# A two-layer recurrent decoder on one core: the second layer's recurrence in a new order of visits, its block transfers cut to the diagonal, and the weight loads on another queue

## The chip, the cores and the metric

The kernel runs on one core of a Trainium2 chip. The metric is the device time of one execution in microseconds: 2776.45 us as the median of three runs (2772.79, 2776.45 and 2785.57). One more execution was profiled; it took 2771.17 us, and its instructions span 2769.4 us.

## The reference, cut to what matters

Layer 0 (an RG-LRU and an HGRN2 group side by side) is left as it is. The change touches layer 1, RWKV-7 time mixing over 1024 positions, 2048 channels in 32 heads of 64, and the last projection with the final norm:

```
def rwkv7_scan(r, decay, k, v, kk, a):
    def step(state, inp):
        r_t, w_t, k_t, v_t, kk_t, a_t = inp
        s_kk = jnp.einsum("bhvk,bhk->bhv", state, kk_t)
        state = (state * w_t[:, :, None, :]
                 - s_kk[..., None] * (kk_t * a_t)[:, :, None, :]
                 + v_t[..., None] * k_t[:, :, None, :])
        y_t = jnp.einsum("bhvk,bhk->bhv", state, r_t)
        return state, y_t
...
    r = x_r @ w_r
    k_raw = x_k @ w_k
    v = x_v @ w_v
...
    y = rwkv7_scan(r, decay, k, v, kk, a)
    mean = jnp.mean(y, axis=-1, keepdims=True)
    var = jnp.mean(jnp.square(y - mean), axis=-1, keepdims=True)
    y = ((y - mean) * lax.rsqrt(var + GN_EPS)).reshape(bsz, s, RW_WIDTH) * lnx_g + lnx_b
    bonus = (jnp.sum(r * k * r_k, axis=-1, keepdims=True) * v).reshape(bsz, s, RW_WIDTH)
    out = ((y + bonus) * gate) @ w_o
```

## The kernel before, in words

The program runs layer 0, then the gates and low-rank parts of layer 1, and from about 1170 us of the profile on the part that the change touches. There the 1024 positions are cut into four quarters of 256 and the 32 heads into eight groups of four, which makes 32 **units**. In a unit the 256 positions of four heads are worked on as chunks of 64 positions, sixteen squares of 64 by 64 in all, so that the recurrence becomes small matrix products.

The work of one unit is written as generators, and each `yield` in them ends one *visit*:

- `stage_g` makes the unit's kr, r and v with 144 matmuls on 256 columns (names `g`). Every matrix value is a sum of two parts, so each product takes three matmuls. One piece of a weight matrix (512 KB, tile `wt`, names `w_kr`, `w_r`, `w_v`, later `w_o`) serves twelve matmuls; `piece` loads it ahead into one of five buffers.
- `stage_a` prepares decays and keys, forms the 128 by 128 products `pa`, masks them into `am`, stores the part that has to be inverted to DRAM (`nd`), and transposes (`pat`, `pbt`).
- `stage_i` reads these blocks back as `nb` (128 partitions of 32 by 32 values) and inverts the 32 blocks by 31 steps on VectorE (`itmp`, `xi`), about sixty short instructions a unit. The result goes to DRAM (`xd`) and comes back as `x32`, in the trace `x<-xd`.
- `stage_l` turns `x32` round on VectorE and joins the blocks to the inverse of a 64 by 64 square with two groups of 32 by 32 matmuls (`pl`, `pl2`).
- `stage_v` makes the centred v (`pvt`) and a first product with it (`pr0`).
- `stage_s` does the recurrence: `p1` in two halves, whose result is copied to `t1` and cast into `uv`; `p2` for even and odd chunks, added into `gm` and `rp` on VectorE; `ph` and `py`; and then four steps of the state, each with eight small matmuls into `ph` and eight into `py` and one VectorE instruction for the state (`sts`, at the last step `sper`).
- `stage_n` norms the result (sum `pvr`), multiplies by the gate and stores it (`y1d`).

The string `program` says in which order one turn of the loop makes these visits: a letter is a stage, the number behind it the distance of its unit from the current one, and a bare number so many sixths of `g` work (six matmuls each). TensorE's instructions are pinned to the order in which they are written. For the other engines a scheduler with its own timing sets the order, and each engine works through its own list in order. At the ends of the quarters `stage_x` makes the next quarter's inputs (names `xm`, `u`) beside the units.

PSUM has eight banks here: two for `g`, two for `pn`, `pb`, `pa`, `pat`, `pbt` (tag `m`), one for `pvt`, `pr0`, `pl`, `pl2` (tag `b`), one for `pvr`, `p1`, `p2` (tag `s`), and one each for `ph` and `py`.

A transfer is issued by the engine named before `.dma_start`, in that engine's order: SyncE (SP) issues the weights and all transfers of `nd`, `nb`, `xd`, `x32` and `y1d`; ScalarE (ACT) issues the reads of decays, a's and gates. `outs` is the last projection: it runs in two halves after the last `g`, with weights `w_o`.

Lines to follow: `pmap` 860, `pin` 873, `load_parts` 918, `piece` 924, `stage_a` 968, its stores of `nd` 1039, `stage_i` 1065 with its reads at 1070 and 1093, `stage_l` 1115, `stage_s` 1157 with the casts at 1169 and 1170, `stage_n` 1227, `outs` 1268, `program` 1351. Matmuls all carry the helper's line 882 (885 for transposes).

Of the kernel before, what the change touches and what calls it, by code (L numbers as in the profile page):

```python
# [19 lines left out]
P = 128  # L20
# [11 lines left out]
def trunk_kernel(ctx: ExitStack, tc: tile.TileContext, I, out, dbg=None):  # L32
# [822 lines left out]
    def eo(t):  # L855
# [6 lines left out]
        m="pn pb pa pat pbt",  # L862
        b="pvt pr0 pl pl2",
        s="pvr p1 p2",
# [8 lines left out]
    pinned = [None]  # L873

    def pin(i):
        if pinned[0] is not None:
            after(i, pinned[0])
        pinned[0] = i
        return i

    def mm(*args, **kw):
        return pin(PE.matmul(*args, **kw))  # L882

    def tr(*args):
        return pin(PE.transpose(*args))
# [30 lines left out]
    order_w = [(j, p_, q) for _ in range(4) for p_ in range(8) for j in range(3) for q in range(4)]  # L916
    loaded = []

    def load_parts(src, name):
        t = wp[0].tile([P, 2, 2, TQ], F32R, tag="wt", bufs=5, name=f"w_{name}")  # L920
        nc.sync.dma_start(t.bitcast(F32), src)
        return t

    def piece(i):

        while len(loaded) < min(i + 4, len(order_w)):
            j, p_, q = order_w[len(loaded)]
            loaded.append(load_parts(wd[p_][j][q], ("kr", "r", "v")[j]))
        return loaded[i][:, 0], loaded[i][:, 1]

    def weights1(dq, kp):
        ts = [load_parts(wod[dq][kp * 2 + q], "o") for q in range(2)]
        return [[t[:, w, k] for t in ts for k in range(2)] for w in range(2)]
# [34 lines left out]
    def stage_a(u):  # L968

        qt, pp_ = u["qt"], u["pp"]  # L970
        kr, rt = u["kr"], u["r"]
# [8 lines left out]
        yield  # L980
        k = spare(1, "k")
        for h_, c1 in two(pp_):
            S.activation(k[:, h_], a[:, h_], AF.Identity, scale=prm["c_k_a"][:, c1], bias=kam1[:, c1])
# [3 lines left out]
        after(S.activation(lamt[:, :, 1:65], ch(cum), AF.Exp, scale=-KAPPA), tabs)  # L987
# [3 lines left out]
        S.activation(li, cum, AF.Exp, scale=KAPPA)  # L991
# [9 lines left out]
        bh, bl = W1("ysq", dtype=F32R, name="bh"), W1("hsl", dtype=F32R)  # L1001
# [23 lines left out]
        nd = dp.tile([NCH * 2 * 4160], F32, tag="nd", bufs=2, name="nd")  # L1025
        ndw = nd.rearrange("(g h e x) -> g h e x", h=2, e=2, x=4160)
        for q in range(2):
# [6 lines left out]
            for h in range(2):  # L1034
# [3 lines left out]
                for e in range(2):  # L1038
                    nc.sync.dma_start(
                        ndw[q * 2:q * 2 + 2, h, 1 - e, 0:4096].rearrange("g (m t) -> m g t", t=64),  # L1040
                        am[q][ur[e], h, e::2, 0:64])
# [22 lines left out]

    def stage_i(u):
# [11 lines left out]
        for m in range(31):  # L1077
# [40 lines left out]
    def stage_l(u):  # L1118
# [36 lines left out]
    def stage_s(u):  # L1155
# [266 lines left out]
```

## Time and profile before

| what | value |
|---|---|
| median of three runs | 2776.45 us |
| the profiled execution | 2771.17 us, span 2769.4 us |
| TensorE busy over the span | 92% |
| VectorE, ScalarE, GpSimd busy | 62%, 44%, 24% |
| granted TensorE clock, mean | 0.972 |
| DMA | 566.50 MB in 531232 packets, 237745 of them under 512 B |

Busy shares are averages over stages with different limits. Matmuls overlap, so a busy TensorE is not one at its peak; what an edit is worth is read from the waits and the starts of single groups in the stage concerned. The share of the chain that ended last is 42% TensorE, 17% DMA and 15% VectorE.

### The profile page before, as it was taken

The numbers are of one execution on the slowest core, as the hardware profiler recorded it, in microseconds if no ns is written. First come the engines' busy times: TensorE is split into PE (matmuls) and PEld (weight loads), VectorE is DVE, ScalarE is ACT, GpSimd is POOL, SyncE is SP. The second block draws the span as 40 slices with busy tenths as digits, with TensorE's granted clock in tenths as the row PEclk, the third lists the DMA queues.
The fourth block names the chain that finished last, engine by engine and source line by source line (L and its number), as shares of the span: only waits on it lengthen the run. The fifth ranks groups of instructions, "written<-read, shape, count | busy, mean of one in ns | idle before, by whom it ended". The sixth has DMA issues, their size and how long they took to land.

```text
span 2769.4 us, 56914 instructions
## 1 busy us (share of the span) xinstructions
PE 2549.4 (92%) x22203; PEld 2214.3 (80%) x22203; DVE 1728.9 (62%) x4058; ACT 1226.1 (44%) x2439; POOL 654.7 (24%) x648
## 2 busy tenths in 40 slices
PE   7999999999999989997988999889998899998988
PEld 6777878788998766586887888778887788887988
DVE  5466566557657586245787676777767777677221
ACT  5466555555444455433345343453434434443221
POOL 2355444451116450111112011121111211110001
PEclk9999999999999999898999999999999999999999
DMA  6576666674564567685667576666765667666574
GB/s 202 170 254 223 217 212 224 222 255 141 190 192 137 178 198 223 207 293 177 191 210 225 183 221 191 201 203 210 227 198 189 208 204 221 202 211 186 170 266 151
DMA packets 531232, 566.50 MB, mean 205 GB/s; under 512 B 237745, under 2 KB 420242, under 8 KB 530962
## 3 DMA queue, kind: packets, MB, share of 16 engines
q1 hardware_dynamic: 473906, 481.50, 55.4%
q10 hardware_dynamic: 56192, 79.19, 8.7%
q8 instruction: 174, 2.85, 0.4%
q0 software_dynamic: 864, 2.18, 0.2%
q14 instruction: 96, 0.79, 0.1%
HBM read 428.52 MB, written 134.22 MB: 203 GB/s over the span
## 4 chain that ended last, share of the span: by engine, by line
PE 42%; DMA 17%; DVE 15%; issue 8%; ACT 6%; POOL 5%; SPq 4%; ACTq 0%; DVEq 0%; POOLq 0%
PE g L882 12%; PE pa L882 3%; DMA wd<-ht 3%; PE acc L882 3%; PE ph L882 3%; PE p L882 3%; POOL ht L382 2%; SPq L1093 2%; DVE xi L1086 2%; DVE itmp L1084 2%; PE py L882 2%; DMA y1d<-gt 2%; DMA x<-xd 2%; DMA nb<-nd 2%; SPq L1070 2%
## 5 line engine op out<-in xcount | busy, mean ns | idle before, releaser
L882 PE MATMUL g<-x,w_kr 128*128 128x256 f32 x1536 | 243.1, 301 | 8.2 <-DMA w_kr<-wd 8.2
L882 PE MATMUL g<-x,w_r 128*128 128x256 f32 x1536 | 247.1, 298 | 2.3 <-DMA w_r<-wd 2.3
L882 PE MATMUL g<-x,w_v 128*128 128x256 f32 x1536 | 232.7, 301 | 12.4 <-DMA w_v<-wd 12.3
L1086 DVE TENSOR_TENSOR xi<-xi,itmp 128x60 f32<-128x60 f32 (+21 forms) x864 | 222.5, 258 | 24.0
L382 POOL TENSOR_TENSOR ht<-ht 128x512 fp32r<-128x512 f32 x128 | 191.7, 1508 | 183.3 <-ACT ht L381 136.4
L1084 DVE TENSOR_TENSOR itmp<-xi,nb 128x60 f32<-128x60 f32 (+21 forms) x864 | 220.5, 255 | 22.5
L882 PEld LDWEIGHTS g<-x,w_kr 128*128 128x128 f32 x1536 | 206.6, 197 | 27.6 <-issue 19.5
L882 PEld LDWEIGHTS g<-x,w_v 128*128 128x128 f32 x1536 | 198.6, 194 | 32.7 <-DMA w_v<-wd 16.0
L882 PEld LDWEIGHTS g<-x,w_r 128*128 128x128 f32 x1536 | 199.6, 191 | 17.5 <-DMA w_r<-wd 2.5
L249 PE MATMUL acc<-wL_o,y 128*128 128x256 f32 x512 | 144.5, 286 | 7.1 <-DVE wL_o L183 7.1
L247 PE MATMUL acc<-wH_o,y 128*128 128x256 f32 x512 | 139.1, 285 | 4.2 <-ACT wH_o L182 2.0
L250 PE MATMUL acc<-wH_o,y 128*128 128x256 f32 x512 | 142.6, 283 | 0.0
L1074 POOL TENSOR_SCALAR xi<-eye 128x256 f32<-128x256 f32 x32 | 27.5, 861 | 469.0 <-DMA xd<-xi 388.6
L381 ACT CAST ht<-ht 128x512 fp32r<-128x512 f32 x128 | 78.2, 617 | 120.1 <-DMA wd<-ht 55.8
L882 PE MATMUL acc<-w_o,y 128*128 128x256 f32 x960 | 119.8, 288 | 7.3 <-DVE y L1263 4.2
L882 PEld LDWEIGHTS acc<-w_o,y 128*128 128x128 f32 x960 | 118.4, 196 | 8.6 <-DVE y L1263 4.9
L882 PE MATMUL p<-am,t 64*64 64x128 f32 x1024 | 73.6, 285 | 52.1 <-ACT uv L1170 52.1
L997 DVE TENSOR_TENSOR P<-r,lam 128x512 f32<-128x512 f32 x32 | 49.7, 1552 | 113.6 <-ACT r L953 113.6
L1036 DVE TENSOR_TENSOR am<-pa,rwm 128x512 f32<-128x512 f32 x128 | 85.4, 687 | 56.3 <-PE pa L882 56.1
L1217 ACT COPY ysb<-py 128x512 f32<-128x512 f32 x32 | 18.8, 587 | 229.2 <-PE py L882 229.2
L833 POOL TENSOR_TENSOR x<-xm,x 128x512 fp32r<-128x512 f32 x48 | 65.6, 1371 | 210.2 <-ACT x L832 210.2
L199 PE MATMUL gr<-g,wL_g 128*128 128x512 f32 x256 | 105.5, 412 | 9.4 <-DVE wL_g L183 9.3
(391 smaller groups left out, 6614.9 us busy)
## 6 DMA issues: line engine op xcount, KB each, us to landing
w_kr<-wd SPq DMA_DIRECT2D x128, 512.0 KB, 6.7
w_r<-wd SPq DMA_DIRECT2D x128, 512.0 KB, 4.1
w_v<-wd SPq DMA_DIRECT2D x128, 512.0 KB, 3.9
wd<-ht SPq DMA_DIRECT2D x96, 512.0 KB, 3.6
w_o<-wod SPq DMA_DIRECT2D x64, 512.0 KB, 3.4
wod<-ht SPq DMA_DIRECT2D x32, 512.0 KB, 3.6
wst_o<-in_ab_w_out_dram SPq DMA_DIRECT2D x64, 256.0 KB, 3.2
wst_g<-in_c_w_g_dram SPq DMA_DIRECT2D x64, 256.0 KB, 3.0
```

The lines of the kernel that those rows point to most:

```text
L199: PE.matmul(ps, l[k], xh[k], start=False, stop=(k == NK - 1))
L247: PE.matmul(o, yH[kt][:, ts_], wh[j], start=(first and tb % 2 == 0), stop=False, skip_group_check=True)
L249: PE.matmul(o, yH[kt][:, ts_], wl[j], start=False, stop=False, skip_group_check=True)
L250: PE.matmul(o, yL[kt][:, ts_], wh[j], start=False, stop=last, skip_group_check=True)
L381: i = S.copy(hl[:, 0].bitcast(F32R), st)
L382: G.tensor_tensor(hl[:, 1].bitcast(F32R), st, hl[:, 0], op=sub)
L833: G.tensor_tensor(xl, x, xh.bitcast(F32), op=sub)
L882: return pin(PE.matmul(*args, **kw))
L1036: V.tensor_tensor(am[q][:, h, :, 0:P], pa.rearrange("p (c t) -> p c t", t=P), rwm.unsqueeze(1).broadcast_to([P, 4, P]), op=mult)
L1070: nc.sync.dma_start(nb[32 * g:32 * g + 32], u["nd"].rearrange("(p x) -> p x", x=2080)[:, 0:2048].rearrange("p (m s) -> p m s", s=64)[:, :, ...
L1084: V.tensor_tensor(t3, xi[:, 0:n, m:m + 1].broadcast_to([P, n, w]), nb[:, m:m + 1, m + 1:32].broadcast_to([P, n, w]), op=mult)
L1086: V.tensor_tensor(xi[:, 0:n, m + 1:32], xi[:, 0:n, m + 1:32], t3, op=add)
```

## The change

- **Order of visits.** The string `program` is new. Small matmuls that stood alone between pieces of `g` work now stand in a row: both halves of `p2`, `ph`, `py` and the first state step; a state step with one half of `pa`, twice; the last state step with `pr0`. With the two groups of `stage_l` these are six places a unit in which matmuls use parts of the array; before there were twelve. In return `g` stands in longer pieces.
- **PSUM.** `p1` and `p2` get two names each, one on tag `s` and one on tag `b`; `pvt` moves to tag `m`.
- **Casts.** Both casts of `p1` into `uv` are done on ACT; before, one was on VectorE.
- **Blocks.** Only the 32 by 32 diagonal blocks are stored to `nd` (eight stores of 16 KB in place of eight of 32 KB), and `nb` is read in one transfer of 512 KB with rows of 4 KB in place of four transfers of 128 KB with rows of 128 B. The number of a square within `xb` and the squares' places in `am` follow.
- **Weight loads.** All of them, `w_o` too, go through `piece`, are issued by ACT in place of SP, and run five pieces ahead in place of four.
- **ACT's order.** Some ACT work of `stage_a` must stand behind the last copy of `pl` (`behind`).
- **Norm.** The store of `y1d` becomes a visit of its own, made one turn later.
- The last unit's `g` work is all done in its own turn.

```diff
@@ -859,9 +859,9 @@
-        m="pn pb pa pat pbt",
-        b="pvt pr0 pl pl2",
-        s="pvr p1 p2",
+        m="pn pvt pb pa pat pbt",
+        b="p1b p2b pr0 pl pl2",
+        s="p1a p2a pvr",
@@ -870,19 +870,25 @@
...
+    pinned = {}
+
+    def pin(f):
...
+    mm, tr = pin(PE.matmul), pin(PE.transpose)
+    last_copy = []
+
+    def behind(i):
+        for c in last_copy:
+            after(i, c)
@@ -913,24 +919,18 @@
-    order_w = [(j, p_, q) for _ in range(4) for p_ in range(8) for j in range(3) for q in range(4)]
+    order_w = [(wd[p_][j][q], ("kr", "r", "v")[j]) for _ in range(4) for p_ in range(8) for j in range(3) for q in range(4)]
+    order_w += [(wod[dq][q], "o") for _ in range(2) for dq in range(4) for q in range(8)]
...
-    def load_parts(src, name):
-        t = wp[0].tile([P, 2, 2, TQ], F32R, tag="wt", bufs=5, name=f"w_{name}")
-        nc.sync.dma_start(t.bitcast(F32), src)
-        return t
-
     def piece(i):
 
-        while len(loaded) < min(i + 4, len(order_w)):
-            j, p_, q = order_w[len(loaded)]
-            loaded.append(load_parts(wd[p_][j][q], ("kr", "r", "v")[j]))
+        while len(loaded) < min(i + 5, len(order_w)):
+            src, name = order_w[len(loaded)]
+            t = wp[0].tile([P, 2, 2, TQ], F32R, tag="wt", bufs=5, name=f"w_{name}")
+            nc.scalar.dma_start(t.bitcast(F32), src)
+            loaded.append(t)
         return loaded[i][:, 0], loaded[i][:, 1]
-
-    def weights1(dq, kp):
-        ts = [load_parts(wod[dq][kp * 2 + q], "o") for q in range(2)]
-        return [[t[:, w, k] for t in ts for k in range(2)] for w in range(2)]
 
     def stage_g(u):
@@ -978,17 +978,20 @@
...
-            S.activation(k[:, h_], a[:, h_], AF.Identity, scale=prm["c_k_a"][:, c1], bias=kam1[:, c1])
+            behind(S.activation(k[:, h_], a[:, h_], AF.Identity, scale=prm["c_k_a"][:, c1], bias=kam1[:, c1]))
...
-        after(S.activation(lamt[:, :, 1:65], ch(cum), AF.Exp, scale=-KAPPA), tabs)
+        i = S.activation(lamt[:, :, 1:65], ch(cum), AF.Exp, scale=-KAPPA)
+        after(i, tabs)
+        behind(i)
...
-        S.activation(li, cum, AF.Exp, scale=KAPPA)
+        behind(S.activation(li, cum, AF.Exp, scale=KAPPA))
@@ -1022,8 +1025,8 @@
 
-        nd = dp.tile([NCH * 2 * 4160], F32, tag="nd", bufs=2, name="nd")
-        ndw = nd.rearrange("(g h e x) -> g h e x", h=2, e=2, x=4160)
+        nd = dp.tile([32 * 1024], F32, tag="nd", bufs=2, name="nd")
+        ndw = nd.rearrange("(q c e u m t) -> q c e u m t", q=2, e=2, u=2, m=32, t=32)
         for q in range(2):
             yield
             pas = [pu("pa") for h in range(2)]
@@ -1035,10 +1038,11 @@
                 pa = pas[h]
                 V.tensor_tensor(am[q][:, h, :, 0:P], pa.rearrange("p (c t) -> p c t", t=P),
                                 rwm.unsqueeze(1).broadcast_to([P, 4, P]), op=mult)
-                for e in range(2):
-                    nc.sync.dma_start(
-                        ndw[q * 2:q * 2 + 2, h, 1 - e, 0:4096].rearrange("g (m t) -> m g t", t=64),
-                        am[q][ur[e], h, e::2, 0:64])
+            for e in range(2):
+                for b in range(2):
+                    r0 = ur[e].start + 32 * b
+                    nc.sync.dma_start(ndw[q, :, 1 - e, b].rearrange("c m t -> m c t"),
+                                      am[q].rearrange("p h (g e) t -> p (h g) e t", e=2)[r0:r0 + 32, :, e, 32 * b:32 * b + 32])
         u.update(pt=pt, am=am, bv=bv, nd=nd, lc=lc)
 
@@ -1062,13 +1066,13 @@
...
 
         nb = W1("nb", bufs=1, shape=(P, 32, 32))
-        for g in range(4):
-            nc.sync.dma_start(nb[32 * g:32 * g + 32], u["nd"].rearrange("(p x) -> p x", x=2080)[:, 0:2048].rearrange(
-                "p (m s) -> p m s", s=64)[:, :, 0:32])
+        nc.sync.dma_start(nb.rearrange("p m s -> p (m s)"),
+                          u["nd"].rearrange("(p x) -> p x", x=1024).unsqueeze(0).broadcast_to([4, 32, 1024]))
@@ -1088,6 +1092,7 @@
                 yield
         nc.sync.dma_start(xd.rearrange("g c x t -> g (c x t)").rearrange("g (b y) -> (g b) y", y=256),
                           xi.rearrange("p j t -> p (j t)"))
+        yield
...
@@ -1133,12 +1138,11 @@
...
-                ce = (c // 2) * 2 + h
-                mm(pl[rb, c * 32:c * 32 + 32], am[ce // 4][ra, c % 2, ce % 4, 32:64], x1[ra, c, :],
+                mm(pl[rb, c * 32:c * 32 + 32], am[c // 4][ra, c // 2 % 2, c % 2 * 2 + h, 32:64], x1[ra, c, :],
...
             rb = slice(ur[h].start + 32, ur[h].start + 64)
-            S.copy(x1[rb].rearrange("p c t -> p (c t)"), pl[rb, 0:256])
+            last_copy[:] = [S.copy(x1[rb].rearrange("p c t -> p (c t)"), pl[rb, 0:256])]
         yield
@@ -1161,19 +1165,19 @@
-            p1 = pu("p1")
+            p1 = pu(("p1a", "p1b")[q])
             for j in range(4):
-                mm(p1[:, j * P:(j + 1) * P], xb[:, q * 4 + j, :], ar[:, :, q * 4 + j, :], start=True, stop=True)
+                mm(p1[:, j * P:(j + 1) * P], xb[:, q * 4 + j % 2 * 2 + j // 2, :], ar[:, :, q * 4 + j, :], start=True, stop=True)
             p1 = p1.rearrange("p (j s c) -> p j s c", s=2, c=64)
             S.copy(t1[:, q * 4:q * 4 + 4], p1[:, :, 0])
-            V.tensor_copy(uv[q][ur[0], 0], p1[ur[0], :, 1])
-            S.copy(uv[q][ur[1], 1], p1[ur[1], :, 1])
+            for e in range(2):
+                S.copy(uv[q][ur[e], e], p1[ur[e], :, 1])
             yield
 
         gm = W1("gm", bufs=1, shape=(P, NCH, 64))
         rp = W1("rp", bufs=1, shape=(P, NCH, 64))
         for e in range(2):
-            p2 = pu("p2")
+            p2 = pu(("p2a", "p2b")[e])
             for g in range(4):
...
-            if e == 0:
-                ph = pu("ph")
...
-                py = pu("py")
...
-                yield
+
+        ph = pu("ph")
...
+        py = pu("py")
...
+        yield
@@ -1242,6 +1245,7 @@
...
+        yield
         nc.sync.dma_start(y1d[qt // 2][pp_ // 2][2 * (pp_ % 2):2 * (pp_ % 2) + 2, :,
                                                  (qt % 2) * TQ:(qt % 2 + 1) * TQ].rearrange("i p t -> p i t"),
...
@@ -1274,16 +1278,15 @@
...
             for kt in range(16):
-                if kt % 4 == 0:
-                    wh, wl = weights1(dq, kt // 4)
-                j = kt % 4
+                wh, wl = piece(12 * n + (hf * 4 + dq) * 8 + kt // 2)
...
                     o = acc[tb // 2][:, (tb % 2) * 256:(tb % 2) * 256 + 256]
-                    mm(o, yH[kt][:, ts_], wh[j], start=(kt == 0 and tb % 2 == 0), stop=False, skip_group_check=True)
-                    mm(o, yH[kt][:, ts_], wl[j], start=False, stop=False, skip_group_check=True)
-                    mm(o, yL[kt][:, ts_], wh[j], start=False, stop=(kt == 15), skip_group_check=True)
+                    mm(o, yH[kt][:, ts_], wh[:, j], start=(kt == 0 and tb % 2 == 0), stop=False, skip_group_check=True)
+                    mm(o, yH[kt][:, ts_], wl[:, j], start=False, stop=False, skip_group_check=True)
+                    mm(o, yL[kt][:, ts_], wh[:, j], start=False, stop=(kt == 15), skip_group_check=True)
...
@@ -1349,8 +1352,8 @@
     program = """
-        a2 s0 2 i1 v1 i1 s0 1 i1 a2 1 i1 s0 1 s0 1 i1 s0 1 v1 1 i1 s0 1 a2 1 i1 s0 1 i1 a2 1 i1 s0 1 i1 s0 n0 1
-        a2 1 i1 a2 1 a2 i2 1 n0 l1 1 i2 a3 l1 3 i2 l1 i2 1 i2 1 a3 i2 1""".split()
+        s0 s0 v1 i1 1 a2 i1 1 n-1 i1 s0 s0 s0 s0 i1 1 i1 1 i1 1 s0 a2 i1 1 i1 1 1 s0 a2 i2 i1 1 i2 1 i2 1 s0 v1
+        i2 a3 2 n0 a2 a2 i2 2 i2 a2 n0 l1 i2 1 i2 2 a3 i2 1 l1 i2 1 1 l1 1 a3 i2 2""".split()
...
-            if s + d == n - 1:
-                left = 21
...
                 fill(k)
-                if s + d == n and left < 97:
+                if s + d == n and left < 99:
...
-                go(t[0], s + int(t[1]))
+                go(t[0], s + int(t[1:]))
...
             prepare(4)
+    go("n", n - 1)
...
-    fill(96 - 80)
+    fill(96 - 83)
```

The next pieces show what stands in a row on an engine, before and after. They are of the twentieth unit.

First TensorE, from the product with the inverse on. `p` and `p1a`, `p1b` are the halves of `p1` where they read `ar` and `xb`; `p`, `p2a`, `p2b` with `am` and `t` are `p2`; "..." stands for matmuls of `g` and for the other half of `pb`. Before:

```order
L882 MATMUL p_22604<-ar,xb 128x128 x4
...
L882 MATMUL pvt<-cent,v 128x128 x4
L882 MATMUL p_22646<-ar,xb 128x128 x4
...
L882 MATMUL pb<-hsl,bdr 128x512
...
L882 MATMUL p_22686<-am,t_22603 64x128 x8
...
L882 MATMUL ph<-uv,am 64x64 x16
L882 MATMUL py<-am,uv 64x64 x16
...
L882 MATMUL p_22749<-am,t_22603 64x128 x8
```

and now:

```order
L878 MATMUL p1a<-ar,xb 128x128 x4
L878 MATMUL p1b<-ar,xb 128x128 x4
L878 MATMUL pvt<-cent,v 128x128 x4
...
L878 MATMUL pb<-bl,bdr 128x512
...
L878 MATMUL p2a<-am,t_22561 64x128 x8
L878 MATMUL p2b<-am,t_22561 64x128 x8
L878 MATMUL ph<-uv,am 64x64 x16
L878 MATMUL py<-am,uv 64x64 x16
L878 MATMUL ph<-sper,gm 64x64 x4
L878 MATMUL py<-rp,sper 64x64 x4
```

The halves of `p1` have become neighbours, on two banks, and `p2`, `ph`, `py` and the first state step are one run without `g` between them.

Next ACT at the same place. `t` and `uv` are the copies out of `p1`, `sqa` the norm of the keys, `w_kr` and `w_r` weight loads. Before:

```order
L1002 CAST bh<-r 128x512
L953 COPY v<-g 128x512
L1008 ACTIVATE sqa<-sqa 128x512
L1168 COPY t_22603<-p_22604 128x256
L1009 ACTIVATE sqa<-sqa 128x512
L1170 COPY uv<-p_22604 64x256
L1234 DMA gt<-gd 128x512
L1106 COPY uv<-pvt 64x256 x4
L1168 COPY t_22603<-p_22646 128x256
L987 ACTIVATE lam<-cum 128x8x64
L1170 COPY uv<-p_22646 64x256
```

and now:

```order
L931 DMA w_kr<-wd_210 128x1024
L1005 CAST bh<-r 128x512
L1011 ACTIVATE sqa<-sqa 128x512
L953 COPY v<-g 128x512
L931 DMA w_r<-wd_211 128x1024
L1012 ACTIVATE sqa<-sqa 128x512
L1172 COPY t_22561<-p1a 128x256
L1174 COPY uv<-p1a 64x256 x2
L1172 COPY t_22561<-p1b 128x256
L1174 COPY uv<-p1b 64x256 x2
L1237 DMA gt<-gd 128x512
L1111 COPY uv<-pvt 64x256 x4
```

Six copies out of `p1` stand together ahead of those out of `pvt`, and weight loads stand among ACT's own work.

Last VectorE, from the end of the inverse to the next one. `itmp` and `xi` are steps of the inverse, `x` is `x32`, `sts` and `sper` the state. Before:

```order
L1084 TENSOR_TENSOR itmp<-xi,nb 128x8
L1086 TENSOR_TENSOR xi<-xi,itmp 128x8
L1221 TENSOR_TENSOR sts<-ph,lc 128x128
L1036 TENSOR_TENSOR am<-pa,rwm 128x4x128 x2
L1221 TENSOR_TENSOR sts<-ph,lc 128x128
L1221 TENSOR_TENSOR sper<-ph,lc 128x128
L997 TENSOR_TENSOR P<-r,lam 128x512
L1124 STREAM_TRANSPOSE x_22454<-x_22399 32x256 x2
L1129 COPY xb<-x_22399 32x8x32 x2
```

and now:

```order
L1088 TENSOR_TENSOR itmp<-xi,nb 128x8
L1090 TENSOR_TENSOR xi<-xi,itmp 128x8
L1224 TENSOR_TENSOR sper<-ph,lc 128x128
L1129 STREAM_TRANSPOSE x_22398<-x_22204 32x256 x2
L1134 COPY xb<-x_22204 32x8x32 x2
L1000 TENSOR_TENSOR P<-r,lam 128x512
```

Behind the last step of the inverse (`xi` of 128x8) stood six instructions that need other engines and `P`; now the last state step alone stands there, and `P` stands behind the transposes.

## Rows read from the trace of the kernel before

**Rows 1.** The page: busy us, share of the span, instructions.
```profile
PE 2549.4 (92%) x22203; PEld 2214.3 (80%) x22203; DVE 1728.9 (62%) x4058; ACT 1226.1 (44%) x2439; POOL 654.7 (24%) x648
```

**Rows 2.** Busy time by stretch: PE, PEld, DVE, ACT, POOL, clock, DMA share, GB/s.
```profile
1428.30:1573.50 145.20, 120.65 (x1382) 108.25 (x1380) 103.66 (x304) 65.61 (x144) 30.91 (x30) 0.92 0.65 201
1573.50:1775.80 202.30, 190.56 (x2348) 169.68 (x2347) 147.39 (x459) 82.02 (x180) 25.02 (x30) 1.00 0.68 206
1775.80:1873.80 98.00, 83.54 (x949) 74.34 (x948) 74.63 (x210) 49.45 (x108) 26.04 (x24) 0.91 0.66 204
2121.00:2218.00 97.00, 83.23 (x957) 73.88 (x956) 73.65 (x204) 47.80 (x104) 25.82 (x24) 0.93 0.63 196
```

**Rows 3.** The key norm's first VectorE instruction, by line, 1310 to 2463 us.
```profile
L1007 DVE TENSOR_SCALAR sqa<-pn x28: 682/684/694, 1310.8 to 2462.4; 128x512 f32<-128x512 f32 x28
```

**Rows 4.** The same line, 1573.5 to 1775.8 us.
```profile
L1007 DVE TENSOR_SCALAR sqa<-pn x6: 683/684/694, 1573.5 to 1775.8; 128x512 f32<-128x512 f32 x6
```

**Rows 5.** TensorE's waits, 1170 to 2770 us: total us, times, longest.
```profile
PE p L882 <- ACT uv L1170: 63.3, 42, 5.4
PE pl L882 <- DVE x L1124: 44.0, 52, 11.6
```

**Rows 6.** TensorE's waits, 1573.5 to 1775.8 us.
```profile
PE p L882 <- ACT uv L1170: 6.5, 7, 1.1
PE pl L882 <- DVE x L1124: 2.6, 10, 0.4
PE g L882 <- DMA w_v<-wd: 2.6, 4, 1.4
```

**Rows 7.** TensorE's waits, 1428.3 to 1573.5 us.
```profile
PE p L882 <- ACT uv L1170: 12.3, 5, 5.4
PE pl L882 <- DVE x L1124: 8.1, 2, 8.0
PE g L882 <- DMA w_v<-wd: 2.0, 1, 2.0
```

**Rows 8.** TensorE's timeline: start us, us, instruction, count.
```profile
1576.94 0.96 PE L882 MATMUL g<-x,w_kr 128*128 128x256 f32 x6
1577.74 0.40 PE L882 MATMUL pb<-bh,bdr 128*128 128x512 f32 x1
...
1591.27 0.98 PE L882 MATMUL g<-x,w_r 128*128 128x256 f32 x6
1592.17 0.45 PE L882 MATMUL ph<-sts,gm 64*64 64x64 f32 x8
1592.46 0.40 PE L882 MATMUL py<-rp,sts 64*64 64x64 f32 x8
1592.79 0.98 PE L882 MATMUL g<-x,w_r 128*128 128x256 f32 x6
```

**Rows 9.** The chain that ended last, 1536 to 1552 us: start us, us.
```profile
1540.23 2.23 DMA xd<-xi
...
1542.51 0.59 SPq L1093
...
1545.10 4.25 DMA x<-xd
...
1549.48 0.44 DVE x L1124
```

**Rows 10.** The tile uv, 1573.5 to 1775.8 us: ns min, median, max.
```profile
L1169 DVE COPY uv<-p x10: 427/427/428, 1575.1 to 1741.8; 64x256 f32<-64x256 f32 x10
L1170 ACT COPY uv<-p x10: 366/366/367, 1575.6 to 1742.2; 64x256 f32<-64x256 f32 x10
```

**Rows 11.** A transfer that ACT issues, line 1234: ns of the issue.
```profile
L1234 ACTq DMA_DIRECT2D gt<-gd x32: 326/326/495, 1174.7 to 2584.4; - x32
```

**Rows 12.** The page's DMA issues: count, KB each, us to landing.
```profile
w_kr<-wd SPq DMA_DIRECT2D x128, 512.0 KB, 6.7
nb<-nd SPq DMA_DIRECT2D x128, 128.0 KB, 3.0
```

**Rows 13.** SP's own waits, 1170 to 2770 us.
```profile
SPq L921 <- PE g L882: 575.2, 219, 12.4
```

More of the change, by code (lines that the diff above doesn't have):

```diff
@@ L870, in pu, with g @@
         return pp[0].tile([P, 512], F32, tag=pmap[use], bufs=pcnt[pmap[use]], name=use)
[L873 to L885, printed above, removed]
+    pinned = {}
+    def pin(f):
+        def g(*args, **kw):
+            i = f(*args, **kw)
+            e = i.ins.engine
+            if e in pinned:
+                after(i, pinned[e])
+            pinned[e] = i
+            return i
+        return g
+    mm, tr = pin(PE.matmul), pin(PE.transpose)
[3 more added lines that the diff above has]
+            after(i, c)
     xb = W1("xb", shape=(P, 8, P))
@@ L970, in stage_a @@
         qt, pp_ = u["qt"], u["pp"]
-        kr, rt = u["kr"], u["r"]
+        kr = u["kr"]
         cum = W1("cum", bufs=2)
@@ L980, in stage_a @@
         yield
+        rt = u["r"]
         k = spare(1, "k")
         for h_, c1 in two(pp_):
-            S.activation(k[:, h_], a[:, h_], AF.Identity, scale=prm["c_k_a"][:, c1], bias=kam1[:, c1])
+            behind(S.activation(k[:, h_], a[:, h_], AF.Identity, scale=prm["c_k_a"][:, c1], bias=kam1[:, c1]))
         V.tensor_tensor(k, kr, k, op=mult)
@@ L1000, in stage_a @@
             V.scalar_tensor_tensor(rt[:, h_], rt[:, h_], prm["c_r_k"][:, c1], k[:, h_], op0=mult, op1=mult)
-        bh, bl = W1("ysq", dtype=F32R, name="bh"), W1("hsl", dtype=F32R)
+        bh, bl = W1("ysq", dtype=F32R, name="bh"), W1("hsl", dtype=F32R, name="bl")
         S.copy(bh, rt)
@@ L1185, in stage_s @@
             yield
-            if e == 0:
-                ph = pu("ph")
-                for c in range(NCH):
-                    for h in range(2):
-                        j = (c // 2) * 2 + h
-                        mm(ph[hr[h], cs(c)], am[c // 4][:, h, c % 4, P:192], uv[c // 4][:, c % 2, j % 4, :],
-                           start=(c == 0), stop=False, skip_group_check=True)
-                py = pu("py")
-                for c in range(NCH):
-                    for h in range(2):
-                        j = (c // 2) * 2 + h
-                        mm(py[hr[h], cs(c)], uv[c // 4][:, c % 2, j % 4, :], am[c // 4][:, h, c % 4, 64:128],
-                           start=(c == 0), stop=False, skip_group_check=True)
-                yield
+        ph = pu("ph")
+        for c in range(NCH):
+            for h in range(2):
+                j = (c // 2) * 2 + h
+                mm(ph[hr[h], cs(c)], am[c // 4][:, h, c % 4, P:192], uv[c // 4][:, c % 2, j % 4, :],
+                   start=(c == 0), stop=False, skip_group_check=True)
+        py = pu("py")
+        for c in range(NCH):
+            for h in range(2):
+                j = (c // 2) * 2 + h
+                mm(py[hr[h], cs(c)], uv[c // 4][:, c % 2, j % 4, :], am[c // 4][:, h, c % 4, 64:128],
+                   start=(c == 0), stop=False, skip_group_check=True)
+        yield
         sts = W1("sts", bufs=1, shape=(P, 4, 2, 64))
@@ L1276, in outs @@
             for kt in range(16):
-                if kt % 4 == 0:
-                    wh, wl = weights1(dq, kt // 4)
-                j = kt % 4
+                wh, wl = piece(12 * n + (hf * 4 + dq) * 8 + kt // 2)
+                j = kt % 2
                 for tb in range(4):
```

## The prediction

> **What bounds the kernel now.** I read the page first: TensorE is busy for 92% of the span, VectorE for 62%, ScalarE (ACT) for 44% [rows 1]. That makes TensorE the engine to watch, and the question is where it is not at its own pace. For that I took stretches [rows 2] and counted units in them with one instruction that stands once in each unit. It starts 28 times between 1310.8 and 2462.4 us, so 27 units take 1151.6 us, 42.65 us each [rows 3]. Where no inputs of a next quarter are made, five units take 202.3 us, 40.5 each, at a clock of 1.00 [rows 4]. In the three stretches beside the making of inputs the clock is 0.91 to 0.93, a mix of the two levels 1.2 and 2.4 GHz, and seven units take 145.2 + 98.0 + 97.0 = 340.2 us, 48.6 each [rows 2]. The other 20 units are then (1151.6 - 340.2) / 20 = 40.6.
>
> The waits come next. TensorE stands before `p1`, whose bank is held by the casts of `uv`, for 63.3 us in all, and before the products with the inverse (`pl`) for 44.0 us [rows 5]. In the five undisturbed units these two and a late weight make 6.5 + 2.6 + 2.6 = 11.7 us, 2.3 a unit [rows 6]; in the first stretch 12.3 + 8.1 + 2.0 = 22.4 us in three units, 7.5 each [rows 7]. VectorE is busy for 147.39 / 5 = 29.5 us of an undisturbed unit and ACT for 82.02 / 5 = 16.4 [rows 2], so no engine but TensorE is near its limit by work alone. VectorE is near it by a chain, below.
>
> **Visits.** A group of six `g` takes 0.80 us from its start to that of the following `pb` in full tiles, and 0.90 us to that of a `ph` in parts of the array; the way back, from `py` to `g`, is 0.33 us, where `ph` to `py` is 0.29 [rows 8]. One visit thus costs 0.10 going in and 0.04 coming out, and I take 0.15 in all. Twelve visits become six: 6 x 0.15 = 0.9 us a unit. But four changes of shape now stand inside a visit (`p2` to `ph`, `py` to a state step, a state step to `pa` twice), each between 0 and 0.10, so the term lies between 0.5 and 0.9. I take 0.7. A rule of the Trainium skill speaks against it (TensorEngine Tiling (Array Packing), Key Properties): changing the tiling mode, not only the tile, drains TensorE, so modes would be counted and not visits, 24 changes before and 16 now, and by half a visit's 0.15 for each change the term would be 8 x 0.075 = 0.6. The rows bear the drain out going in, by the 0.10; for a change inside a visit none of them has a price.
>
> **Banks and casts.** The halves of `p1` and of `p2` get two banks, so the second half need not wait for the copies of the first; the same waits cannot come back at `p1`, they can only move to the first user of either bank. The cast that leaves VectorE frees 2 x 0.427 = 0.86 us there a unit and costs ACT 2 x 0.366 = 0.73 [rows 10]. ACT has 24 us a unit free, which hides that as long as copies do not queue up; uncovered it is the 0.73.
>
> **Weight loads.** Twelve issues a unit go from SP to ACT. An issue takes ACT 0.326 us [rows 11], so 12 x 0.326 = 3.9 us a unit, hidden in the same free time: 16.4 + 0.7 + 3.9 = 21.0 of 40. Such a load lands 6.7 us after its issue [rows 12], and TensorE works through a piece, two groups of six, in 40.5 / 12 = 3.4 us on the mean and in 2 x 0.80 = 1.6 us where `g` stands unbroken [rows 8]. Four pieces in between are 13.5 us and 6.4 us, so there is ample time on the mean and none to spare in a dense row of `g`. SP now stands 575.2 us in 219 waits for `g` to free a buffer [rows 13], with the blocks' transfers queued behind. This standing moves to ACT, where copies, casts and exponentials are queued behind it. It does no harm where these need matmuls that come later in TensorE's order than the one waited for, which holds for copies out of `p1`, `pvt` and `ph`; it does harm to the decays' exponentials, whose users are VectorE and GpSimd. I price it at 0, with the upper end in the rival on ACT.
>
> **Blocks.** Eight stores of half the size, no price. Four reads of `nb` with 3.0 us to landing become one of 512 KB, for which the nearest rows are that 3.0 and the 6.7 of a weight piece of equal size [rows 12]. It lies between the reads of `x32`, ahead of it on SP, and the first step of the inverse; VectorE meanwhile has the transposes, `P` and the norm. I take 4.5 and cost 0; at 6.7, uncovered by 2 us, it would add 2 us to VectorE's loop. The Trainium skill has a rule against just this form (DMA: Bandwidth & Descriptors, Rules for kernel authors): an outermost broadcast of c copies keeps the whole transfer on at most c engines, here 4 of 16. With its 27 GiB/s an engine that is 128 KB in about 4.5 us of moving alone (estimate), and the read would land at some 6.5 us, near the upper end; no run here shows a read of that form.
>
> **What is late next.** The chain shows what VectorE's order now leaves bare. From the start of the inverse's way to DRAM to the first transpose of what came back it is 1549.48 - 1540.23 = 9.25 us: 2.23 for the store, issues of 0.59, 4.25 for the reads [rows 9]. Before, VectorE had two masks, three state steps and `P` to do in that time; now only `sper` stands there, and it waits for the transposes with all else behind them. So VectorE's loop is 29.5 - 0.86 + 9.25 = 37.9 us. TensorE's own is 40.5 - 2.3 - 0.7 = 37.5. The two meet, and neither is reached exactly, since each still waits for the other at the masks and the state steps. I add 0.9 to the longer (a choice, of the size of one wait in [rows 6]) and take 38.8 a unit, 1.7 less than 40.5. In the stretches VectorE's work is 103.66 / 3 = 34.6, 74.63 / 2 = 37.3 and 73.65 / 2 = 36.8 [rows 2]; with 9.25 - 0.86 added that is 43.0, 45.7 and 45.2, by units 44.4. I take 44.5, 4.1 less than 48.6. The norm's store a turn later, `behind` and the last projection's loads are hidden by TensorE's `g` and cost 0.
>
> **The sum.** 20 x 1.7 = 34 and 7 x 4.1 = 29. The remaining five units, at both ends, have 0.7 x 5 = 3.5 from visits, and their waits: by rows 6 and 7 the 27 units hold some 20 x 1.3 + 7 x 4.1 = 55 of the 63.3 and 20 x 0.5 + 7 x 2.7 = 29 of the 44.0, which leaves 23, and half of that, 12, goes. Together 78.5 us off the profiled execution's 2771.2: 2693 us. That execution lies 5.3 us under the median of the runs, 0.2%, which I don't add.
>
> **Rivals.**
> - VectorE takes the place entirely: its loop keeps the 9.25 us and waits for masks and state steps besides. Units go to 39.8 and stretches to 47.0: 20 x 0.7 + 7 x 1.6 + 12 = 37 us less, 2734 us. For it speaks that nothing fills the gap; against it that its work alone is far from 40.
> - The chain gets shorter, since no weight load stands between its transfers on SP. At the 3.0 of a small read in place of 4.25 and one issue of 0.59 it is 2.23 + 0.59 + 3.0 = 5.8 us. Then TensorE's 37.5 decides (20 x 3.0 = 60) and the stretches fall to 41.0 (7 x 7.6 = 53): with 15.5 at the ends 128 us less, 2643 us. Against it: the four reads still follow each other at 0.59.
> - Slower: ACT is held in its order. `bh` waits for VectorE's `r`, and a weight load and the copies out of `p1` stand behind it. In a dense row of `g` a load has no time to spare, so a hold of 4 us makes TensorE 4 us late. At once a unit that is 32 x 4 = 128 us against a gain of 78: 2821 us. It decides from 78 / 32 = 2.5 us a unit on. Against it: ACT is idle for half of a unit.
> - The change does not do what it says: waits only move from `uv` to the transposes, visits cost by changes of shape and not by their number, and units stay at 40.5: 2771 us.
>
> **How the numbers follow.** The forecast has 0.50, VectorE in its place 0.17, the shorter chain 0.15, ACT's hold 0.10, no change 0.08. What a measurement of this kernel can tell from no change is about 0.5%, 14 us. The first three are faster: 0.82; 0.08 within; 0.10 slower. The range leaves out ACT's hold, half of the no-change case and the far end of the shorter chain: 2630 to 2765. It holds the 2 us of a late `nb` (32 x 2 = 64 us, 2757).
>
> **What would show it.** Right: the rows `p` behind `uv` are gone or below 10 us; units of about 39 us where the clock is full and about 44.5 in the stretches; VectorE's longest wait is for the reads of `x32`, several us in each unit; six `g` to a group in parts still at 0.90. Wrong: TensorE's waits for `w_kr`, `w_r`, `w_v` of over 20 us (ACT held); waits of VectorE for `nb` of over 1 us a unit (the broadcast); TensorE waiting for `pl` as long as before, with units above 40 (no net gain); or units below 38 with VectorE hardly waiting (the shorter chain).

## The result: 7% slower, and VectorE stands for the blocks

The changed kernel takes 2973.74 us (median of four runs, 2962.09 to 2979.2), the one before 2776.81 (its profiled execution counted in). The ratio is 1.0699, 95% interval 1.0674 to 1.0725. The forecast was 2693 us. The profiled execution took 2962.09 us, 190.9 more than that of before.

First the page, the line of busy time, and of the chain that ended last the shares by engine and the first shares by line:

```profile
PE 2562.4 (87%) x22203; PEld 2255.3 (76%) x22203; DVE 1645.2 (56%) x3994; ACT 1245.6 (42%) x2503; POOL 659.0 (22%) x648
...
PE 30%; DMA 29%; DVE 19%; issue 9%; POOL 5%; ACT 4%; SPq 3%; ACTq 0%; DVEq 0%; POOLq 0%
DMA nb<-nd 14%; PE g L878 7%; DVE itmp L1088 3%; DVE xi L1090 3%; DMA wd<-ht 3%; PE acc L878 3%; POOL ht L382 2%; DMA nd<-am 2%; SPq L1098 2%; PE pa L878 2%; DMA y1d<-gt 2%; PE gr L199 1%; DMA yst<-y1d 1%; PE ph L878 1%; DMA xd<-xi 1%
```

Every engine works about as long as in [rows 1], and VectorE 84 us less; the time is added standing. One transfer, the read of `nb`, is 14% of the chain, more than any line of an engine.

The unit's marker answers [rows 3, 4]; then three stretches answer [rows 2] (columns as there), two quiet ones and one in which inputs are made:

```profile
L1010 DVE TENSOR_SCALAR sqa<-pn x28: 677/683/693, 1327.9 to 2642.8; 128x512 f32<-128x512 f32 x28
```

```profile
L1010 DVE TENSOR_SCALAR sqa<-pn x5: 677/683/684, 1673.8 to 1857.2; 128x512 f32<-128x512 f32 x5
```

```profile
1723.00:1768.00 45.00, 36.53 (x451) 33.09 (x452) 25.74 (x90) 16.98 (x38) 4.32 (x7) 0.94 0.62 184
1768.00:1858.00 90.00, 79.23 (x956) 72.99 (x956) 53.50 (x182) 34.08 (x77) 10.15 (x13) 0.92 0.62 186
1858.00:1966.00 108.00, 81.68 (x932) 73.82 (x932) 72.14 (x220) 50.49 (x112) 26.54 (x25) 0.81 0.61 184
```

27 units take 1314.9 us, 48.7 each in place of 42.65, which is 163 of the 191 us. Four quiet units take 183.4 us, 45.9 each in place of 40.5. TensorE's granted clock falls with its standing: 0.92 to 0.94 where it was 1.00, and 0.81 where it was 0.91 to 0.93.

The waits of VectorE and of TensorE, 1170 to 2770 us (engine, what it starts, what it waits for: total us, times, longest):

```profile
DVE xi L1084 <- DMA nb<-nd: 333.8, 32, 16.6
DVE x L1129 <- DMA x<-xd: 155.1, 22, 11.2
```

```profile
PE pl L878 <- DVE x L1129: 110.6, 33, 16.0
PE p1a L878 <- ACT xb L1156: 87.7, 17, 8.9
PE pbt L878 <- ACT ar L1053: 31.6, 11, 3.8
PE p2a L878 <- ACT uv L1174: 17.7, 10, 3.6
PE g L878 <- DMA w_v<-wd: 15.8, 5, 5.0
```

VectorE stands 10.4 us a unit for `nb`, over ten times the 1 us that the prediction named as its sign of a slow broadcast. Before, by the same view, the tile `nb` was waited for in 18 units:

```profile
  DMA nb<-nd: 29.8, 18
```

The waits of `p1` behind `uv` of [rows 5] are gone as foreseen. TensorE now stands for the products with the inverse, 110.6 us in place of 44.0, and 87.7 us for `xb`, a copy on ACT that itself stands for VectorE (72.2 us, for `ysq`); TensorE's wait for it is 5.8 us once the broadcast is out (the first run below).

One unit shows how it comes. First SP's issues, then VectorE (start us, us, instruction, in brackets the standing before it):

```profile
1793.34 2.68 SPq L1098 DMA_DIRECT2D x<-xd  x4
1796.12 0.55 SPq L1074 DMA_DIRECT2D nb<-nd  x1
```

```profile
1790.25 0.29 DVE L1224 TENSOR_TENSOR sper<-ph,lc 128x128 f32<-128x128 f32 x1 [0.76 <-PE ph L878]
1799.18 0.90 DVE L1129 STREAM_TRANSPOSE x<-x 32x256 f32<-32x256 f32 x2 [8.64 <-DMA x<-xd]
...
1801.22 0.67 DVE L1244 TENSOR_TENSOR ysq<-ysb,ysq 128x512 f32<-128x512 f32 x1
1809.90 0.25 DVE L1084 SCALAR_TENSOR_TENSOR xi<-nb,xi 128x31 f32<-128x31 f32 x1 [8.01 <-DMA nb<-nd]
```

From the issue of `nb` at 1796.12 to its first use it is 13.8 us; over the 32 units, read in the same way, the median is 13.6 (11.1 to 15.1). Before it was 5.4, with VectorE at other work for most of it. The gap for `x32` of 8.64 us was foreseen; that a second of 8.01 stands close behind it was not. 8.64 + 8.01 + some 26.7 us of work (53.50 / 2) is 43.4 of the unit's 45.

### The profile page after: what moved, and what is told of

Read it like the earlier page. It is cut to its first block, busy times and chain, and to the rows that moved or that the text cites. A ratio compares the mean times of both kernels' runs of the same rounds, so it can differ in the third digit from the quotient of the medians.

```text
span 2960.4 us, 56761 instructions
## 1 busy us (share of the span) xinstructions
PE 2562.4 (87%) x22203; PEld 2255.3 (76%) x22203; DVE 1645.2 (56%) x3994; ACT 1245.6 (42%) x2503; POOL 659.0 (22%) x648
## 4 chain that ended last, share of the span: by engine, by line
PE 30%; DMA 29%; DVE 19%; issue 9%; POOL 5%; ACT 4%; SPq 3%; ACTq 0%; DVEq 0%; POOLq 0%
DMA nb<-nd 14%; PE g L878 7%; DVE itmp L1088 3%; DVE xi L1090 3%; DMA wd<-ht 3%; PE acc L878 3%; POOL ht L382 2%; DMA nd<-am 2%; SPq L1098 2%; PE pa L878 2%; DMA y1d<-gt 2%; PE gr L199 1%; DMA yst<-y1d 1%; PE ph L878 1%; DMA xd<-xi 1%
## 5 line engine op out<-in xcount | busy, mean ns | idle before, releaser
L878 PE MATMUL g<-x,w_v 128*128 128x256 f32 x1536 | 250.5, 318 | 15.9 <-DMA w_v<-wd 15.8
L878 PEld LDWEIGHTS g<-x,w_v 128*128 128x128 f32 x1536 | 219.1, 214 | 39.1 <-DMA w_v<-wd 18.3
L878 PE MATMUL g<-x,w_r 128*128 128x256 f32 x1536 | 228.4, 299 | 1.0 <-DMA w_r<-wd 1.0
L878 PE MATMUL g<-x,w_kr 128*128 128x256 f32 x1536 | 223.5, 298 | 5.2 <-DMA w_kr<-wd 5.2
L1084 DVE SCALAR_TENSOR_TENSOR xi<-nb,xi 128x31 f32<-128x31 f32 (+3 forms) x128 | 32.7, 256 | 335.9 <-DMA nb<-nd 333.8
L878 PEld LDWEIGHTS g<-x,w_r 128*128 128x128 f32 x1536 | 196.1, 193 | 22.7 <-issue 15.8
L1006 POOL TENSOR_TENSOR bl<-r,bh 128x512 fp32r<-128x512 f32 x32 | 40.7, 1272 | 440.4 <-ACT bh L1005 421.9
L878 PE MATMUL pl<-x,am 32*32 32x32 f32 x1024 | 30.4, 205 | 110.9 <-DVE x L1129 110.6
L878 PE MATMUL p1a<-ar,xb 128*128 128x128 f32 x256 | 47.2, 343 | 87.7 <-ACT xb L1156 87.7
L1129 DVE STREAM_TRANSPOSE x<-x 32x256 f32<-32x256 f32 x64 | 27.8, 434 | 167.5 <-DMA x<-xd 155.1
L878 PE MATMUL pa<-P,BK 64*128 64x128 f32 x1024 | 112.5, 287 | 3.9 <-DVE BK L1019 1.8
```

What stands on the lines that cost most here:

```text
L878: i = f(*args, **kw)
L1006: G.tensor_tensor(bl, rt, bh.bitcast(F32), op=sub)
L1084: V.scalar_tensor_tensor(xi[:, 0, m + 1:32], nb[:, m, m + 1:32], xi[:, 0, m:m + 1], xi[:, 0, m + 1:32], op0=mult, op1=add)
```

## The experiments

All were timed in three rounds beside the kernel before; ratios are to that, with 95% intervals. "Four reads" means the compact blocks of the change, read plainly.

**The broadcast alone out.**

```diff
-        nc.sync.dma_start(nb.rearrange("p m s -> p (m s)"),
-                          u["nd"].rearrange("(p x) -> p x", x=1024).unsqueeze(0).broadcast_to([4, 32, 1024]))
+        for g in range(4):
+            nc.sync.dma_start(nb[32 * g:32 * g + 32].rearrange("p m s -> p (m s)"),
+                              u["nd"].rearrange("(p x) -> p x", x=1024))
```

> The changed kernel with the 32 by 32 blocks read back in four plain transfers of 128 KB (rows of 4 KB) in place of one broadcast transfer of 512 KB. Theory (the broadcast read lands some 13 us after its issue and VectorE stands for it): VectorE's wait for nb falls from 334 us to under 40, units of the quiet stretch from 44 to 45 us to 38 to 40, the time to 2690 to 2750 us. Rival (the loss lies in the order of visits and in ACT's queue, and nb only shows where it is noticed): the wait moves to x or to the weights and the time stays above 2900 us.

2719.93 us, 0.9822 (0.9791 to 0.9854). The same 512 KB from the same addresses in four transfers is 254 us faster than in one (243 by the two ratios, each to the kernel before as it was timed beside the run), and the change then gains. The time is as expected; the wait is 45.5 us where under 40 was. VectorE's rows, and the transfers' median time to landing:

```profile
DVE x L1130 <- DMA x<-xd: 208.9, 27, 10.9
...
DVE xi L1085 <- DMA nb<-nd: 45.5, 13, 8.3
```

```profile
nb<-nd SPq DMA_DIRECT2D x128, 128.0 KB, 4.6
x<-xd SPq DMA_DIRECT2D x128, 32.0 KB, 3.7
```

**And the weights back on SP.**

```diff
-            nc.scalar.dma_start(t.bitcast(F32), src)
+            nc.sync.dma_start(t.bitcast(F32), src)
```

> As the run before, and the weight loads are issued by SP again, still five pieces ahead. Theory: with the broadcast gone the place of issue matters little, within 15 us of the run before, or some 10 to 40 us slower since SP stands for buffers with the reads of x32 and nb behind it. Rival (ACT's queue is what costs): 50 us or more faster than the run before.

2696.56 us, 0.9730 (0.9690 to 0.9770), 23 us faster than the run before and on the same chip. Both expectations missed: ACT's queue does cost, half of what its rival said. How, the rows show; here VectorE, TensorE and the landings:

```profile
DVE x L1130 <- DMA x<-xd: 138.7, 28, 8.5
DVE xi L1085 <- DMA nb<-nd: 95.6, 30, 8.0
```

```profile
PE g L878 <- DMA w_v<-wd: 26.0, 11, 5.0
PE pl L878 <- DVE x L1130: 20.3, 9, 8.7
```

```profile
nb<-nd SPq DMA_DIRECT2D x128, 128.0 KB, 4.1
x<-xd SPq DMA_DIRECT2D x128, 32.0 KB, 2.2
```

With weights on ACT hardly a weight is late (1.7 us of such waits in all, against 27.7 here), but `x32` lands 3.7 us after issue in place of 2.2. From the issue of the inverse's store to the first transpose it is 9.65 us against 7.3, by the medians of 32 units, and TensorE's wait for `pl` is 54.8 against 20.3. VectorE's wait for `nb` goes the other way, 45.5 against 95.6.

**The broadcast in the kernel before.** The diff is the change's block part alone: `nd`, its stores, the read, and the two index lines in `pl` and `p1`.

> The kernel before with the block part of the change alone: compact blocks, stored in eight pieces of 16 KB, and read back in one broadcast transfer. Theory: each unit gets a wait of VectorE for nb of 5 to 8 us, of which the order of before hides part, so 80 to 200 us slower than before: 2855 to 2975 us. Rival (the broadcast is harmless, the order of visits is the cause): within 20 us of before.

3011.08 us, 1.0878 (1.0842 to 1.0914): slower than expected, and than the whole change. Issue to first use is 13.6 us again. VectorE:

```profile
DVE xi L1080 <- DMA nb<-nd: 279.1, 31, 12.1
```

and TensorE:

```profile
PE g L882 <- DMA w_v<-wd: 154.1, 25, 8.3
PE p L882 <- ACT uv L1169: 65.1, 45, 5.7
```

Here weight pieces, issued by SP in the same queue as the read, come late as well, 154.1 us in all for `w_v`. In the next run, which differs in the read alone, no wait for `w_v` is listed; in the changed kernel, where ACT issues the weights but the order differs too, it is 15.8.

**The same with four plain reads** (the read as in the first experiment).

> The kernel before with compact blocks, read back in four plain transfers. Theory: within 25 us of before, rather faster, since rows of 4 KB replace rows of 128 B: 2750 to 2785 us. Rival (the compact stores themselves cost, by waiting for both masks of a half): as slow as the run with the broadcast.

2749.07 us, 0.9933 (0.9909 to 0.9956). The compact blocks gain 19 us, and the broadcast costs 262 in this kernel, 254 (by ratios 243) in the other.

**Two copies in each of two transfers.**

```diff
+        for g in range(2):
+            nc.sync.dma_start(nb[64 * g:64 * g + 64].rearrange("p m s -> p (m s)"),
+                              u["nd"].rearrange("(p x) -> p x", x=1024).unsqueeze(0).broadcast_to([2, 32, 1024]))
```

> The changed kernel (weights on ACT) with the blocks read back in two broadcast transfers, each of two copies and 256 KB. If a broadcast keeps a transfer on as many DMA engines as it has copies, each engine carries as much per transfer as with four copies (128 KB), and the reads land as late as the single one or later: VectorE waits 300 us or more for nb, time 2960 to 3200 us. If the size of one transfer is what made it late, half the size lands in about half the time: wait about 120 us, time 2780 to 2850 us.

3115.31 us, 1.1243 (1.1203 to 1.1283). Half the size per transfer makes it worse, so size is not the cause, and the fewer copies, the slower, as the first of the two cases had it. From the issue of the first read to the first use it is 19.4 us (median; 15.3 to 23.0), and VectorE:

```profile
  DMA nb<-nd: 457.9, 31
```

**Half the rows by broadcast, half plainly.**

```diff
+        nc.sync.dma_start(nbx[:, 0:512], ndx[:, 0:512].unsqueeze(0).broadcast_to([4, 32, 512]))
+        for g in range(4):
+            nc.sync.dma_start(nbx[32 * g:32 * g + 32, 512:1024], ndx[:, 512:1024])
```

> The changed kernel (weights on ACT) with half of each block's rows read by a broadcast of four copies (256 KB) and the other half by four plain reads of 64 KB. From issue to the first step of the inverse it is 13.6 us with the whole in one broadcast and 8.0 us with four plain reads. If the bytes that each of a few DMA engines has to carry set the landing, half the bytes end about half-way: 10 to 11.5 us, time 2800 to 2890 us. If the broadcast form has a fixed price whatever its size, it stays at 13 us or more and the time above 2940 us.

2797.05 us, 1.0111 (1.0079 to 1.0142), VectorE's wait 164.6 us, issue to first use 7.7 us, less than expected. The first steps read only the half that comes by broadcast (in some units they start before the last plain read is issued), so the 7.7 us are those of 256 KB in four copies: a little over half of 13.6, and no fixed price of the form. The 8.0 us of four plain reads, from which the 10 to 11.5 were worked out, were no landing; VectorE is mostly at other work until then. The loss is 77 of 254 us, less than half. That VectorE's other work covers the first few microseconds would explain it and was not tried apart.

**The order of before, all else as in the fastest.** The string `program` of before, with one `i1` and one `n0` more.

> Four plain reads of the blocks, weights on SP five ahead, two banks for p1 and p2 and both casts on ACT, as in the fastest run so far, but the visits in the order of before (with one more visit for the inverse and for the store of the norm): only the order differs. Theory of the prediction (six visits less are worth about 0.7 us a unit in TensorE, and the rest of the gain is waits that the new order removes): 20 to 45 us slower than the run with the new order, 2717 to 2742 us. Rival (the gain is in the banks and casts, the new order gives nothing because it leaves VectorE standing for x32 and nb): within 10 us, 2687 to 2707 us, or faster.

2725.95 us, 0.9844 (0.9812 to 0.9877): with the new order the kernel is 1.14% or some 30 us faster, as expected. But little of it comes from the units. In the two profiled executions, one a run and on different chips, all `g` work of the units runs from 1166.6 to 2444.5 us with the old order and from 1167.5 to 2440.9 with the new, 4.5 us or 0.14 a unit apart; the first 576 matmuls of `outs` behind it take 23.5 us more with the old order:

```profile
L878 PE MATMUL g<-w_o,y x576: 277/283/682, 2446.3 to 2583.0; 128*128 128x256 f32 x192
```

```profile
L878 PE MATMUL g<-w_o,y x576: 278/283/681, 2443.6 to 2556.8; 128*128 128x256 f32 x192
```

(old order, then new). In the kernel before the same work takes 115.1 us, from 2514.1 to 2629.2. This run keeps the numbers by which the changed kernel fills the last turns with `g` (99 and 96 - 83), chosen for the new order, so it is not only the order that differs there, and the 30 us can't be put down to the order of visits. TensorE's waits, summed over that view, are 93 us with the old order and 106 with the new. Banks, casts, the fifth piece and the smaller edits (ACT's order, the norm's store, the last unit's `g`) together are worth 0.9933 - 0.9844, 25 us; in the units' `g` work, which was 1174.5 to 2490.0 us in the run with the old banks, they make 38 us.

**Reads of `x32` and `nb` on two queues**, every second one on ACT (`(nc.sync, nc.scalar)[g % 2]`), weights on SP.

> As the fastest run so far (four plain reads, weights on SP, new order), with two of the four reads of x32 and two of nb issued by ACT, so that four issues of 0.6 us on SP become two. If VectorE's standing for x32 and nb (139 and 96 us in that run) sets a unit's length: 1.2 us less for each, 20 to 45 us faster, 2650 to 2677 us. If ACT's copies queued behind these waits cost more: slower by 10 us or more.

2685.73 us, 0.9703 (0.9671 to 0.9735), by the ratios 7 us less than on SP alone, short of what was expected. Run a second time:

> The run with split queues once more, beside the one with four pieces ahead: 2675 to 2697 us if it repeats.

2688.79 us, 0.9725 (0.9697 to 0.9753). The time repeats, but both intervals overlap that of SP alone (0.9730, 0.9690 to 0.9770), so no gain is shown. VectorE's waits only changed places, 92.6 us for `x32` and 128.5 for `nb` (the first of the two runs). The other two variants:

> Four plain reads, weights on SP, new order, with all four reads of x32 issued by ACT and all of nb by SP, so that neither stands behind the other. If issuing one behind the other keeps VectorE waiting: its two waits (139 + 96 us with both on SP, 93 + 129 us with both split) fall below 190 us together, time 2660 to 2685 us. If ACT stands for the landing of xd with its own copies queued behind: 2690 us or more.

2699.81 us, 0.9745 (0.9722 to 0.9768), the waits 121.5 + 110.7 us: no gain. `x32`, now on another queue than the weights, lands in 4.0 us.

> As the run with split queues (weights on SP, reads of x32 and nb split over SP and ACT), with weights four pieces ahead as before in place of five. SP stands over 600 us in waits for a buffer in these kernels. If being five ahead makes these waits hold the small transfers up: 10 to 25 us faster, 2660 to 2675 us. If it is what keeps weights in time: TensorE's waits for w appear and it is 10 to 40 us slower. Within 10 us of 2686: the fifth piece does not matter.

2685.97 us, 0.9704 (0.9685 to 0.9723): a fifth piece ahead does not matter.

## Why the prediction was wrong, point by point

**Blocks: the step that failed.** It said: "I take 4.5 and cost 0; at 6.7, uncovered by 2 us, it would add 2 us to VectorE's loop". The read took 13.6 us from issue to use, and VectorE stood 10.4 us a unit for it. The fault is the upper end. It came from a weight piece of equal size, which lands in 6.7 us [rows 12]; an equal size bounds nothing when the form differs, and no row of before showed the form. As the trace bore neither end, the range should not have been closed by the nearest row. The plain reads, the two copies and the halves show that the broadcast form and the bytes in it are the cause, not the size of a transfer, the order or ACT. Nor is the rest of the term 0: with plain reads VectorE still stands 1.4 us a unit for `nb` with the weights on ACT and 3.0 with them on SP, where it was 0.9 before.

The Trainium skill's rule on it (DMA: Bandwidth & Descriptors, Rules for kernel authors) was quoted in the prediction and given no case of its own. Its direction is what the runs bear out: two copies are slower than four, and four slower than transfers whose outermost dimension is 32 partitions. The figure worked out from it, 4.5 us of moving, is a third of what was measured.

The records of single packets in the trace, which no view lists, show why. The read is 128 packets of 4 KB. As one broadcast of four copies they run 2.8 at a time on the mean: four for 42% of the time, and more than four for under 3% of it. As two broadcasts of two copies it is 1.5 at a time, two for 56% and more than two for under 2%, though two transfers are under way. As four plain reads it is 5.7, with up to 16 at once and more than 16 for 1%. A single packet takes much the same in all three (0.23, 0.20 and 0.24 us). So the form holds the read to as many packets at once as it has copies, and a second read of the same form adds none. From the first packet's start to the last one's end it is 10.7 us with four copies (128 x 0.234 / 2.8), 17.0 with two and 5.3 with plain reads; the first starts 2.0, 1.7 and 1.4 us after the issue (medians of 32 units). The estimate's 4.5 us for 32 packets on each of four engines is 0.14 us a packet and four at a time without a pause; measured are 0.23 us and 2.8 at a time. That the missing share is taken by weights on the same engines is likely, but the records name no engine, and it was not tried apart.

**Visits: mis-sized, and hardly seen in a unit's length.** 0.7 us a unit of TensorE's time was forecast. At full clock, from the start of the last `g` ahead of a visit to that of the first behind it, less the 0.12 us from one `g` to the next, the twelve visits of the old order take 13.2 us a unit and the six of the new one 11.9 (medians, 1300 to 2380 us of the runs with old and new order): 1.3 us, above the 0.5 to 0.9 that was allowed. The price going in is as it was read, 0.21 us from a `g` to a group in parts against 0.12, in both orders. A change of shape inside a visit costs as much as the way back to `g` (`p2b` to `ph` 0.20, `py` to `pa` 0.15). What was left out is that neighbours of one shape run side by side: `py` with `pr0`, and `p2a` with `p2b` in the lines below. The prediction's marker, 0.90 us from six `g` to a group in parts, reads 0.80 here; in a long row six `g` take 0.72, so this is not the price gone.

Yet a unit's `g` work got only 0.14 us shorter. Of the 1.3 us a unit, 42 us in all, 25 went into waits of TensorE up to the last `g` (94 us against 69; for late weights 27.7 against 1.6). The forecast of the order's total came near by luck: most of the 30 us lies in the last turns. TensorE with the new order:

```profile
1738.87 0.87 PE L878 MATMUL g<-x,w_kr 128*128 128x256 f32 x6
1739.67 0.76 PE L878 MATMUL p2a<-am,t 64*64 64x128 f32 x10
1740.17 0.33 PE L878 MATMUL p2b<-am,t 64*64 64x128 f32 x2
1740.27 0.28 PE L878 MATMUL p2a<-am,t 64*64 64x128 f32 x2
...
1741.20 1.15 PE L878 MATMUL ph<-uv,am 128*64 128x64 f32 x32
1742.18 1.10 PE L878 MATMUL py<-am,uv 128*64 128x64 f32 x32
1743.21 0.45 PE L878 MATMUL ph<-sper,gm 64*64 64x64 f32 x8
1743.52 0.45 PE L878 MATMUL py<-rp,sper 64*64 64x64 f32 x8
```

**Banks and casts: right in kind.** The row `p` behind `uv` is gone, and what is left has moved to `p2a`, as was said: 17.7 us in the changed kernel, 7.4 with plain reads and the weights on SP. With the casts, the fifth piece and the smaller edits this is worth 25 us; alone it was not timed.

**Weight loads: mis-sized.** Priced at 0, they cost 23 us, and not as the rival on ACT had it. That rival wanted late weights; without the wait for the very first piece these are 17.0 us in the changed kernel, 17.9 in the one before and 1.7 with plain reads. What came later was `x32`. It lands in 2.2 to 3.0 us in the four runs whose weights share its queue (the kernel before among them) and in 3.7 and 4.0 in the two where they don't, with either engine issuing it. Whether that is because the loads no longer wait their turn behind the small transfers, or because two queues share the engines, stays open.

**What is late next: the wait right, the total in part luck.** VectorE's gap for `x32` was foreseen at 9.25 us and is 10.2 in the changed kernel, 7.3 in the faster one. The sum of 78.5 us is about what the change gives without the broadcast and with the weights on SP (2696.56 against 2693); with ACT as issuer, which is what was forecast, it gives 48. And terms of the sum were off in both directions: VectorE's work in a quiet unit is 26.7 us where 28.6 was counted, and 3.0 us a unit of waiting for `nb` were left out.

**The rivals.** None had the broadcast as its mechanism. The one that ended slower had another cause, and its 2821 us lay 153 under the result.

## What to carry to other kernels

A transfer whose form is new to a kernel is bounded by no row of another form, not even by one of the same size; where a rule speaks against the form, that is a rival with a chance of its own; here its price was three times what the rule's figure gave. Joining four reads into one saved three issues of half a microsecond here and cost 8 us a unit; when a read stands on the loop of an engine that has just been left bare, each microsecond of it counts. And when a large bundle of edits loses, take out one transfer before doubting the rest: here the rest gained 1.8%. Last, look where in the program a gain lies before dividing it by the units: here most of the 30 us between the two orders came after the units.

## What the runs showed of the hardware

- One read of 512 KB by a broadcast of four copies takes 13.6 us from issue to use, the four plain reads of the same data land in 3.3 to 4.6 each; two broadcasts of two copies take 19.4, half the bytes in four copies 7.7.
- Packets of 4 KB take 0.20 to 0.24 us each in these reads. With four copies no more than four run at a time but for under 3% of it (2.8 on the mean), with two copies two (1.5), though there are two such transfers; plain reads have up to 16 (5.7).
- The page gives no time to landing for any transfer of the four programs that read `nb` by broadcast, wholly or in half; it has to be read from the issue and the first user.
- Such a read also delays what is queued behind it: TensorE waited 154.1 us in all for `w_v` on the same queue, and not at all in the same kernel with plain reads.
- Reads of 32 KB land in 2.2 to 3.0 us when the 512 KB loads are issued by the same engine (four runs) and in 3.7 and 4.0 when another issues them (two runs).
- At full clock a matmul in parts of the array starts 0.21 us after a `g`, where the next `g` starts after 0.12; two groups of one shape on different parts run side by side.
